# S5 head group: impulse responses on column quarters, spread through DRAM; state products ahead of time, shifted states in segments

## The chip, the cores and the metric

The kernel runs on one core of a Trainium2 chip. The time is the device time of one execution in microseconds. Before the change it is 2622.58 us, the median of three runs (2621.67 to 2623.46).

## The reference, cut to what matters

One layer of a streaming encoder for 384 tokens, a prompt of 256 and 8 running streams of 16: a SwiGLU feed-forward part (FFN), a mixer of two head groups, a second FFN, norms between. All of it is float32. The mixer projects the normed input once and splits the result into the SSD group (convolution, chunked scan) and the S5 group. The S5 group has 64 channel groups of 16 channels; each drives a complex diagonal state of 64 numbers:

```python
step = exp(log_step);  lb = exp((lam_re + 1j*lam_im) * step)      # 64 groups x 64 states
q    = (lb - 1) / lam                                              # zero-order hold
bu   = einsum('blgh,gnh->blgn', u, q[..., None] * b)
bu[:, 0] += lb * h0                                                # running streams have a state
h[t] = lb * h[t-1] + bu[t]                                         # associative scan over tokens
y    = real(einsum('blgn,ghn->blgh', h, c)) + d * u
```

The outputs are y, and the last state h of the prompt and of each stream. Then y goes through GELU, a gated linear layer and a norm into the output projection.

## The kernel before, in words

**The main products.** Every weight matrix is cut in blocks of 128 columns. `linear` (line 74) makes one output tile of 128 x 384. Its weights come in units of up to 8 blocks of 128 x 128: SP's queue loads `raw`, ScalarE rounds it to `wh` (line 55), VectorE makes the rest `wl` (line 56), and TensorE runs three products per block (lines 86 to 88). `raw` has four buffers, `wh` and `wl` three each. After every unit `c.tick()` is called.

**The FFN** (line 191) takes gate and up tiles in chunks of 11, 11, 11 and 10 for the first FFN. Per tile VectorE takes the gate product out (line 213), ScalarE applies SiLU (214), GpSimd multiplies by the norm factor (`f_g`, line 215), VectorE multiplies with the up product (218). After the tiles of a chunk come the down products (225), without GpSimd work.

**Work beside it.** `s5_prepare` (line 268) and `s5_run` (481) are generators, advanced by `tick`: at each third tick in the first FFN, from its chunk 1 on, at each tick in the mixer. That fixes the order in which instructions are traced. The order on each engine is then made by a planner that simulates the program with costs of its own: it takes the ready instruction that was traced earliest. So small operations that are ready early run long before their place in the trace, in gaps of their engine; but on the chip each engine and each queue works through its fixed order, and an instruction that waits holds up all behind it.

**s5_prepare** computes, from the parameters alone, the matrices of a scheme in steps of four tokens, in eight parts (`e`) of four groups of 128 rows (`l`), and puts them in DRAM: `s5m` holds per part five matrices, the two of the input side (`rt`, lines 453 to 457), the two of the output side (`cl`, 396 to 414), and the direct one (`tt`, 430 to 450): the effect of an input on the outputs of the same step of four tokens. For the direct one, `bbd` holds q times b as a block-diagonal operand, repeated for the four tokens, 128 columns wide; eight products per part (line 433) give the impulse responses for token distances 0 to 3, and ten multiply-adds on VectorE with a mask (447) put each at its place by distance. `s5e` holds the phases (`ph`, 459 to 477): powers of the unit numbers by doubling, on GpSimd, one buffer, stored by GpSimd's queue.

**s5_run** works part by part, `front(e)` and `back(e)`. `load_in` fetches the input matrices (`bdr`, one buffer) and the phases, `load_out` the output matrices (`bdo`, two buffers), all on SP's queue. In `front`, `px` (529) multiplies the input; VectorE turns it by the phases (549 to 554); GpSimd makes the decay mask `d0` (538) and the initial states times the fourth power, `lh` (547), and adds `lh` at the starts of the streams (558); VectorE scans (559); the result is turned back by products on VectorE (566) and GpSimd (567) and written to `hin` one step later (570, 571: one operation for the prompt and one for the streams); GpSimd takes out the last states, `fin` (572, 573), and puts zeros and initial states at the starts (574, 575). In `back`, `py` (582) multiplies the step inputs and `hin` by the output matrices, and ScalarE applies GELU. `psa` is a pool of four PSUM banks for all of this.

Of the kernel before, what the change touches and what calls it, by code (L numbers as in the profile page):

```python
# [267 lines left out]
def s5_prepare(c, a, late):  # L268
# [11 lines left out]
    c.s5e = c.dram.tile([8, P, 2, 4, 96], F32, name="s5_phases")  # L280
    with tc.tile_pool(name="s5p", bufs=1) as pool:
# [39 lines left out]
        l4 = c.const.tile([P, 32, 2], F32, name="s5l4")  # L321
        v.tensor_copy(l4[:, :, 0], lpr[:, :, 4])
        v.tensor_copy(l4[:, :, 1], lpi[:, :, 4])
        c.s5l4 = l4
# [52 lines left out]
        bbd = [t(f"bbd{i}", (P, 4, 2, 4, 16)) for i in range(2)]  # L377
        dd = t("dd", (P, 32))
        with tc.issue_after(late.ins):
            for i in range(2):  # L380
                gp.memset(bbd[i], 0.0)
            gp.dma_start(dd, a["s5d"])
        for e in range(8):
# [56 lines left out]
            tt = t("tt", (P, 4, 64))  # L440
            v.tensor_mul(
                tt, dd[:, ls].unsqueeze(2).to_broadcast([P, 4, 64]), c.ieq.unsqueeze(1).to_broadcast([P, 4, 64])
            )
# [15 lines left out]
            ph = t("ph", (P, 2, 4, 96))  # L459
# [12 lines left out]
            for z in (er, ei):  # L472
# [3 lines left out]
                )  # L476
            gp.dma_start(c.s5e[e], ph)
# [3 lines left out]
def s5_run(c, a, o, u, v5, gc):  # L481
# [10 lines left out]
    with tc.tile_pool(name="s5r", bufs=1, side="right") as pool:  # L492
# [4 lines left out]
        fin = pool.tile([P, 2, 32, 9], F32, name="s5fin")  # L497
# [11 lines left out]
        def load_in(e):  # L509
# [3 lines left out]
            phs[e] = pool.tile([P, 2, 4, 96], F32, tag="ph", name=f"ph{e}", bufs=2)  # L513
# [7 lines left out]
        def front(e):  # L521

            ls = slice(4 * e, 4 * e + 4)
            ph = phs[e]
            px = []
            for i in range(2):
# [11 lines left out]
            gp.tensor_mul(  # L538
                d0,
                c.s5dec[:, ls].unsqueeze(2).to_broadcast([P, 4, 96]),  # L540
                c.scanmask.unsqueeze(1).to_broadcast([P, 4, 96]),
            )
            lh = pool.tile([P, 2, 4, 8], F32, tag="lh", name=f"lh{e}")
            lt = pool.tile([P, 2, 4, 8], F32, tag="lt", name=f"lt{e}")
            l4 = [c.s5l4[:, ls, i].unsqueeze(2).to_broadcast([P, 4, 8]) for i in range(2)]
            he = [h0[:, i, ls, :] for i in range(2)]
            cmul(gp, lh[:, 0], lh[:, 1], he[0], he[1], l4[0], l4[1], lt[:, 0], lt[:, 1])
            gr, gi, a1, a2 = t("gr", 3), t("gi", 3), t("a1"), t("a2")
# [14 lines left out]
            hin = [t("gr", 3), t("gi", 3)]  # L563
            for i in range(2):
# [4 lines left out]
                hi4, b14, b24 = (z[:, :, 64:96].rearrange(smp, b=8) for z in (hin[i], b1, b2))  # L569
# [45 lines left out]
        nc.sync.dma_start(o["s5"], fin)  # L615
# [350 lines left out]
def trunk(ctx: ExitStack, tc: tile.TileContext, a, o):  # L966
# [23 lines left out]
    cst = c.const.tile([P, 684], F32, name="cst")  # L990
# [3 lines left out]
    c.smask, c.ieq, c.scanmask, c.seqm = cst[:, 512:516], cst[:, 516:580], cst[:, 580:676], cst[:, 676:684]  # L994
# [91 lines left out]
def _shape_constants():  # L1086
# [8 lines left out]
            (k // 16) % 4 == np.arange(4)[None, :],  # L1095
            k % 64 == np.arange(64)[None, :],
# [26 lines left out]
def layout(i):  # L1123
# [47 lines left out]
    d = a["s5_d"].reshape(32, 2, 16).transpose(1, 2, 0)  # L1171
    out["s5d"] = np.broadcast_to(d[:, None], (2, 4, 16, 32)).reshape(P, 32)
# [47 lines left out]
```

## Time and profile before

| | us |
|---|---|
| median of three runs | 2622.58 |
| the profiled execution | 2624.0 |
| its span, first to last instruction | 2622.2 |
| TensorE busy | 2570.5 |
| VectorE busy | 1387.7 |
| ScalarE busy | 926.5 |
| GpSimd busy | 658.8 |

The profile is of one execution. TensorE's mean granted clock over it is 0.991 of full speed. A product's record is longer than its share of the time, since products overlap: the main products are recorded with some 327 ns and begin every 0.16 us. Products of float32 operands that are not rounded, as in the S5 part, are two records each. The first FFN lasts to about 1060 us, the S5 parts run from 1160 to 1270 us.

### The profile page before, as it was taken

How to read it: one execution, taken by the hardware profiler on the slowest of the kernel's cores; microseconds unless marked ns; L12 is line 12 of the kernel's file. 1: busy time of each engine (PE TensorE's matmuls, PEld its weight loads, DVE VectorE, ACT ScalarE, POOL GpSimd, SP SyncE). 2: the span in 40 equal slices, each digit the busy share in tenths (PEclk: the TensorE clock that was granted, in tenths of full speed). 3: DMA queues.
4: the chain of work that ended last, by engine and by line, in shares of the span. 5: the costliest groups of instructions: out<-in, count | busy, mean ns of one | idle time of the engine just before them, and what ended most of it. 6: DMA issues, size and time to landing. Idle time of an engine off the chain costs nothing.

```text
span 2622.2 us, 39628 instructions
## 1 busy us (share of the span) xinstructions
PE 2570.5 (98%) x15873; PEld 2546.2 (97%) x15873; DVE 1387.7 (53%) x1964; ACT 926.5 (35%) x1180; POOL 658.8 (25%) x1012
## 2 busy tenths in 40 slices
PE   8989999999999999999899999999999999999997
PEld 8989999999999999988899999999999999999997
DVE  7744466564444445568878865444344444444443
ACT  6322332223323335332445644333223332233343
POOL 1573283121100003027566531100000010000112
PEclk9999999999999999999999999999999999999998
DMA  6444564454444436467455544444444444444443
GB/s 204 151 129 140 165 200 149 138 160 135 133 127 147 136 121 186 150 163 159 122 170 167 166 151 136 137 136 129 135 139 137 136 130 133 141 137 137 131 133 107
DMA packets 147001, 380.41 MB, mean 145 GB/s; under 512 B 46080, under 2 KB 51360, under 8 KB 146816
## 3 DMA queue, kind: packets, MB, share of 16 engines
q1 hardware_dynamic: 133456, 344.28, 43.3%
q0 software_dynamic: 11344, 30.72, 3.8%
q10 hardware_dynamic: 2016, 2.87, 0.3%
q8 instruction: 124, 2.03, 0.3%
q14 instruction: 61, 0.50, 0.1%
HBM read 354.60 MB, written 20.05 MB: 143 GB/s over the span
## 4 chain that ended last, share of the span: by engine, by line
PE 86%; DVE 6%; POOL 4%; issue 1%; DMA 1%; ACT 1%; SPq 0%; DVEq 0%; ACTq 0%; POOLq 0%
PE f_pd L86 9%; PE f_pd L88 9%; PE f_pd L87 9%; PE f_pg L86 8%; PE f_pg L87 8%; PE f_pg L88 8%; PE f_pu L88 8%; PE f_pu L86 8%; PE f_pu L87 8%; PE p L87 2%; PE p L86 2%; PE p L88 2%; DVE wl L56 2%; PE u L87 1%; PE u L88 1%
## 5 line engine op out<-in xcount | busy, mean ns | idle before, releaser
L55 ACT CAST wh<-raw 128x1024 fp32r<-128x1024 f32 (+3 forms) x668 | 658.4, 986 | 1450.9 <-PE f_pd L87 417.2
L56 DVE TENSOR_TENSOR wl<-raw,wh 128x1024 fp32r<-128x1024 f32 (+3 forms) x668 | 788.5, 1181 | 678.9 <-ACT wh L55 672.0
L88 PE MATMUL f_pu<-n_h,wl 128*128 128x384 f32 x1360 | 445.7, 328 | 8.1 <-DVE wl L56 8.1
L215 POOL TENSOR_TENSOR f_g<-f_g,n_r 128x384 f32<-128x384 f32 x86 | 130.4, 1516 | 1271.7 <-ACT f_g L214 1271.6
L86 PE MATMUL f_pd<-f_hh,wh 128*128 128x384 f32 x1376 | 448.1, 326 | 0.0
L87 PE MATMUL f_pd<-f_hl,wh 128*128 128x384 f32 x1376 | 448.1, 326 | 0.0
L88 PE MATMUL f_pd<-f_hh,wl 128*128 128x384 f32 x1376 | 448.1, 326 | 0.0
L86 PE MATMUL f_pg<-n_h,wh 128*128 128x384 f32 x1360 | 445.0, 327 | 2.6 <-DVE f_g L213 2.6
L86 PE MATMUL f_pu<-n_h,wh 128*128 128x384 f32 x1360 | 445.5, 328 | 0.0
L87 PE MATMUL f_pu<-n_l,wh 128*128 128x384 f32 x1360 | 445.1, 327 | 0.0
L87 PE MATMUL f_pg<-n_l,wh 128*128 128x384 f32 x1360 | 444.1, 327 | 0.0
L88 PE MATMUL f_pg<-n_h,wl 128*128 128x384 f32 x1360 | 444.0, 326 | 0.0
L88 PEld LDWEIGHTS f_pu<-n_h,wl 128*128 128x128 f32 x1360 | 258.5, 190 | 8.7 <-DVE wl L56 8.7
L86 PEld LDWEIGHTS f_pg<-n_h,wh 128*128 128x128 f32 x1360 | 257.5, 189 | 3.0 <-issue 2.9
L87 PEld LDWEIGHTS f_pd<-f_hl,wh 128*128 128x128 f32 x1376 | 260.0, 189 | 0.0
L88 PEld LDWEIGHTS f_pd<-f_hh,wl 128*128 128x128 f32 x1376 | 260.0, 189 | 0.0
L86 PEld LDWEIGHTS f_pd<-f_hh,wh 128*128 128x128 f32 x1376 | 260.0, 189 | 0.0
L86 PEld LDWEIGHTS f_pu<-n_h,wh 128*128 128x128 f32 x1360 | 258.5, 190 | 0.1
L87 PEld LDWEIGHTS f_pu<-n_l,wh 128*128 128x128 f32 x1360 | 258.4, 190 | 0.1
L87 PEld LDWEIGHTS f_pg<-n_l,wh 128*128 128x128 f32 x1360 | 257.6, 189 | 0.1
L88 PEld LDWEIGHTS f_pg<-n_h,wl 128*128 128x128 f32 x1360 | 257.6, 189 | 0.0
L218 DVE TENSOR_TENSOR f_h<-f_pu,f_g 128x384 f32<-128x384 f32 x86 | 47.8, 556 | 163.2 <-PE f_pu L88 121.4
(481 smaller groups left out, 3133.0 us busy)
## 6 DMA issues: line engine op xcount, KB each, us to landing
raw<-in_wg_dram SPq DMA_DIRECT2D x170, 512.0 KB, 3.6
raw<-in_wu_dram SPq DMA_DIRECT2D x170, 512.0 KB, 3.6
raw<-in_wd_dram SPq DMA_DIRECT2D x80, 448.0 KB, 3.4
raw<-in_win_dram SPq DMA_DIRECT2D x64, 512.0 KB, 4.0
raw<-in_wd_dram SPq DMA_DIRECT2D x80, 320.0 KB, 3.0
raw<-in_wd_dram SPq DMA_DIRECT2D x48, 384.0 KB, 3.2
raw<-in_wout_dram SPq DMA_DIRECT2D x32, 512.0 KB, 3.8
raw<-in_wd_dram SPq DMA_DIRECT2D x16, 512.0 KB, 3.5
```

The source lines that it names most:

```text
L55: nc.scalar.copy(wh[:, :nk, :], raw[:, :nk, :])
L56: nc.vector.tensor_sub(wl[:, :nk, :], raw[:, :nk, :], wh[:, :nk, :].bitcast(F32))
L86: nc.tensor.matmul(ps, wh[:, i, :], xh, start=first, stop=False)
L87: nc.tensor.matmul(ps, wh[:, i, :], xl, start=False, stop=False)
L88: nc.tensor.matmul(ps, wl[:, i, :], xh, start=False, stop=last)
L215: on_pool = nc.gpsimd.tensor_mul(g, g, r)
L218: nc.vector.tensor_mul(halves(h), straight(pu), halves(g))
```

## The change

The direct matrix: `bbd` is no longer repeated for four tokens, so each product has 32 columns of weights. The four groups of a part are put on the four column quarters of the array, and write the four quarters of the partitions of one PSUM bank. Two operations of VectorE take the result to `kt`, with the diagonal term for distance 0. GpSimd's queue stores `kt` in DRAM (`kd`), and after a yield eight transfers from DRAM to DRAM copy it to the places by distance in the direct matrix, which one transfer has filled with zeros ahead.

The state products: `lh` is made in `s5_prepare`, on GpSimd, from a load of the initial states, and travels as 8 more columns of the phases.

In `s5_run`: ScalarE makes `d0` in four operations per part; VectorE adds `lh`; `hin` has segments of five, the state before a step and the four of the step, so that one operation of VectorE per part writes all; ScalarE copies each last state of a segment to the start of the next, the initial states to the streams' starts, and the last states to `fin`, which has two buffers now and is stored part by part on SP's queue. `py` reads the first four of each segment.

```diff
@@ s5_prepare @@
-    c.s5e = c.dram.tile([8, P, 2, 4, 96], F32, name="s5_phases")
+    c.s5e = c.dram.tile([8, P, 2, 4, 104], F32, name="s5_phases")
...
-        bbd = [t(f"bbd{i}", (P, 4, 2, 4, 16)) for i in range(2)]
-        dd = t("dd", (P, 32))
+        bbd = [t(f"bbd{i}", (P, 4, 2, 16)) for i in range(2)]
+        dd = t("dd", (P, 8))
+        zero = t("zero", (P, 256))
...
+        gp.dma_start(
+            c.s5m[:, :, 4].rearrange("e p l x -> p e (l x)"), zero.unsqueeze(1).to_broadcast([P, 8, 256])
+        )
+        kd = c.dram.tile([8, P, 64], F32, name="k_dram")
         for e in range(8):
...
-                m4 = [mm[pr].unsqueeze(2).to_broadcast([64, 4, 4, 16]) for mm in m]
-                v.tensor_sub(bbd[0][pr, :, g], m4[0], m4[1])
-                v.tensor_add(bbd[1][pr, :, g], m4[2], m4[3])
+                v.tensor_sub(bbd[0][pr, :, g], m[0][pr], m[1][pr])
+                v.tensor_add(bbd[1][pr, :, g], m[2][pr], m[3][pr])
             yield
-            kp = c.psa.tile([P, 4, 64], F32, tag="aux", name=f"kp{e}")
-            for l in range(4):
-                for i in range(2):
+            kp = c.psa.tile([P, 512], F32, tag="aux", name=f"kp{e}")[:, :64]
+            for i in range(2):
+                for l in range(4):
                     nc.tensor.matmul(
-                        kp[:, l, :],
-                        bbd[i][:, l].rearrange("p g s h -> p (g s h)"),
+                        kp[32 * l : 32 * l + 32, :],
+                        bbd[i][:, l].rearrange("p g h -> p (g h)"),
...
-            for b in range(4):
-                for k in range(b + 1):
-                    dst = tt[:, :, 16 * b : 16 * b + 16]
-                    v.scalar_tensor_tensor(
-                        dst, kp[:, :, 16 * k : 16 * k + 16], c.smask[:, b - k : b - k + 1], dst, op0=ALU.mult, op1=ALU.add
-                    )
-            gp.dma_start(c.s5m[e, :, 4], tt)
-            yield
+            kt = t("kt", (P, 64), bufs=2)
+            v.scalar_tensor_tensor(kt[:, 0:16], c.ieq, dd[:, e : e + 1], kp[:, 0:16], op0=ALU.mult, op1=ALU.add)
+            v.tensor_copy(kt[:, 16:64], kp[:, 16:64])
+            gp.dma_start(kd[e], kt)
+            yield
+
+            for s in range(4):
+                for g in range(2):
+                    gp.dma_start(
+                        c.s5m[e, :, 4].rearrange("(g s h) l x -> g s l h x", g=2, s=4)[g, s][:, :, 16 * s :],
+                        kd[e].rearrange("(l g h) x -> g l h x", l=4, g=2)[g][:, :, : 64 - 16 * s],
+                    )
...
+            he = t("he", (P, 2, 4, 8))
+            gp.dma_start(he, a["s5h0"][:, :, ls, :])
+            l4 = [lp[:, ls, 4].unsqueeze(2).to_broadcast([P, 4, 8]) for lp in (lpr, lpi)]
+            cmul(gp, er[:, :, 96:], ei[:, :, 96:], he[:, 0], he[:, 1], l4[0], l4[1], y1[:, :, 0:8], y2[:, :, 0:8])
             gp.dma_start(c.s5e[e], ph)
@@ s5_run, front @@
-            gp.tensor_mul(
-                d0,
...
-            cmul(gp, lh[:, 0], lh[:, 1], he[0], he[1], l4[0], l4[1], lt[:, 0], lt[:, 1])
+            for l in range(4):
+                nc.scalar.activation(d0[:, l, :], c.scanmask, AF.Copy, scale=c.s5dec[:, 4 * e + l : 4 * e + l + 1])
...
-                gp.tensor_add(s0, s0, lh[:, i])
+                v.tensor_add(s0, s0, lh[:, i])
...
+            fin = pool.tile([P, 2, 4, 9], F32, tag="fin", name=f"fin{e}", bufs=2)
+            hin = [pool.tile([P, 4, 24, 5], F32, tag=f"h{i}", name=f"hin{e}_{i}", bufs=2) for i in range(2)]
+            seg = "p l (s k) -> p l s k"
             for i in range(2):
                 b1, b2 = t("a1"), t("a2")
                 v.tensor_mul(b1, hs[i], ph[:, 0])
                 gp.tensor_mul(b2, hs[1 - i], ph[:, 1])
...
-                v.tensor_tensor(hin[i][:, :, 1:64], b1[:, :, 0:63], b2[:, :, 0:63], op=op)
-                v.tensor_tensor(hi4[:, :, :, 1:4], b14[:, :, :, 0:3], b24[:, :, :, 0:3], op=op)
-                gp.tensor_tensor(fin[:, i, ls, 0:1], b1[:, :, 63:64], b2[:, :, 63:64], op=op)
-                gp.tensor_tensor(fin[:, i, ls, 1:9], b14[:, :, :, 3], b24[:, :, :, 3], op=op)
-                gp.memset(hin[i][:, :, 0:1], 0.0)
-                gp.tensor_copy(hi4[:, :, :, 0], h0[:, i, ls, :])
+                gp.memset(hin[i][:, :, 0, 0], 0.0)
+                nc.scalar.copy(hin[i][:, :, 16:24, 0], h0[:, i, ls, :])
+                v.tensor_tensor(hin[i][:, :, :, 1:5], b1.rearrange(seg, k=4), b2.rearrange(seg, k=4), op=op)
+                nc.scalar.copy(hin[i][:, :, 1:16, 0], hin[i][:, :, 0:15, 4])
+                nc.scalar.copy(fin[:, i], hin[i][:, :, 15:24, 4])
+            nc.sync.dma_start(o["s5"][:, :, ls, :], fin)
             return hin
@@ s5_run, back @@
-                for f, mv in ((2, v5[:, 4 * e + l, :]), (0, hin[0][:, l, :]), (1, hin[1][:, l, :])):
+                for f, mv in ((2, v5[:, 4 * e + l, :]), (0, hin[0][:, l, :, 0:4]), (1, hin[1][:, l, :, 0:4])):
```

The rest of the diff follows from this: the mask of the ten multiply-adds leaves the constants, `s5d` is laid out by channel, `s5l4` and the one store of `fin` at the end go.

## Rows read from the trace of the kernel before

**Rows 1.** The page, busy time of TensorE: us (share of span) xrecords.

```profile
PE 2570.5 (98%) x15873; PEld 2546.2 (97%) x15873; DVE 1387.7 (53%) x1964; ACT 926.5 (35%) x1180; POOL 658.8 (25%) x1012
```

**Rows 2.** Windows: length, busy us PE, PEld, DVE, ACT, POOL; clock, DMA share, GB/s.

```profile
1160.00:1280.00 120.00, 107.12 (x718) 104.39 (x717) 93.96 (x159) 37.51 (x46) 80.10 (x167) 0.96 0.69 153
100.00:203.00 103.00, 94.88 (x555) 94.29 (x554) 44.98 (x70) 29.45 (x36) 80.38 (x269) 0.95 0.44 142
203.00:1150.00 947.00, 947.00 (x5868) 943.52 (x5867) 492.11 (x675) 307.64 (x385) 199.93 (x264) 1.00 0.50 149
```

**Rows 3.** TensorE's waits, whole span: who for whom: total us, times, longest.

```profile
PE f_pu L88 <- DVE wl L56: 8.1, 2, 5.3
PE py L582 <- DVE gr L571: 5.0, 3, 1.9
...
PE px L529 <- DMA bdr<-s_mats: 4.0, 2, 2.0
```

**Rows 4.** Timeline of TensorE, one block of line 433: start, us, record, [idle before].

```profile
354.60 1.89 PE L433 MATMUL kp<-cl,bbd 128*128 128x64 f32 x16
356.31 0.41 PE L86 MATMUL f_pg<-n_h,wh 128*128 128x384 f32 x1
```

**Rows 5.** Timeline of TensorE, po products, and pd products on column halves.

```profile
1306.58 1.85 PE L814 MATMUL po<-ct,hT 128*128 128x16 f32 x16
1308.29 0.47 PE L815 MATMUL po<-ct,s 128*128 128x128 f32 x2
...
1320.20 0.88 PE L792 MATMUL pd<-lt,xdt 128*64 128x128 f32 x12
1321.01 0.43 PE L88 MATMUL xs<-n_h,wl 128*128 128x384 f32 x1
```

**Rows 6.** Groups by line, GpSimd's wb loads: busy us, mean ns, idle before.

```profile
L394 POOL DMA_DIRECT2D wb<-w_dram x32 | 19.7, 622 | 0.6 <-DMA w_dram<-ws 0.6
```

**Rows 7.** DMA issues, 40 to 700 us, tt's store: KB, us to landing.

```profile
s_mats<-tt POOLq DMA_DIRECT2D x8, 128.0 KB, 2.8
```

**Rows 8.** Timeline of ScalarE and of GpSimd at one f_g, FFN chunk 1.

```profile
365.13 0.53 ACT L214 ACTIVATE f_g<-f_g 128x384 f32<-128x384 f32 x1 [3.71 <-DVE f_g L213]
...
368.55 1.01 POOL L215 TENSOR_TENSOR f_g<-f_g,n_r 128x384 f32<-128x384 f32 x1
```

**Rows 9.** Timelines, FFN chunk 0: two f_g on ScalarE and GpSimd, phases, TensorE.

```profile
135.50 0.52 ACT L214 ACTIVATE f_g<-f_g 128x384 f32<-128x384 f32 x1
...
147.45 0.10 POOL L462 MEMSET ph<- 128x4 f32 x1 [2.10 <-DMA s_phases<-ph]
...
147.63 0.20 POOL L260 TENSOR_TENSOR ph<-ph,ur 128x4 f32<-128x4 f32 x1
...
150.43 0.99 POOL L215 TENSOR_TENSOR f_g<-f_g,n_r 128x384 f32<-128x384 f32 x1
...
171.82 0.53 ACT L214 ACTIVATE f_g<-f_g 128x384 f32<-128x384 f32 x1 [0.29 <-DVE f_g L213]
...
186.37 0.99 POOL L215 TENSOR_TENSOR f_g<-f_g,n_r 128x384 f32<-128x384 f32 x1
...
191.81 0.69 PE L88 MATMUL f_pu<-n_h,wl 128*128 128x384 f32 x1 [5.33 <-DVE wl L56]
```

**Rows 10.** Groups of GpSimd, 1160 to 1270 us, line 567.

```profile
L567 POOL TENSOR_TENSOR a<-gr,ph 128x384 f32<-128x384 f32 x8 | 10.3, 1293 | 0.8 <-DVE gr L571 0.3
...
L567 POOL TENSOR_TENSOR a<-gi,ph 128x384 f32<-128x384 f32 x8 | 8.3, 1037 | 1.7 <-DVE gi L559 1.7
```

**Rows 11.** Groups of VectorE, 1160 to 1270 us, line 570.

```profile
L570 DVE TENSOR_TENSOR gr<-a,a 128x252 f32<-128x252 f32 x8 | 7.6, 952 | 9.1 <-POOL a L567 9.1
...
L570 DVE TENSOR_TENSOR gi<-a,a 128x252 f32<-128x252 f32 x8 | 3.3, 418 | 2.8 <-POOL a L567 2.6
```

**Rows 12.** Timeline of ScalarE, a small cast.

```profile
1154.95 0.24 ACT L670 CAST dar<-da 128x48 fp32r<-128x48 f32 x1 [0.38 <-DVE da L666]
```

**Rows 13.** Timeline of SP's queue, eight gc transfers.

```profile
1199.45 6.26 SPq L591 DMA_DIRECT2D gc<-gv  x8
```

More of the change, by code (lines that the diff above doesn't have):

```diff
@@ L320, in s5_prepare @@
         c.s5dec = dec
[L321 to L324, printed above, removed]
         qr, qi, den, nr = t("qr"), t("qi"), t("den"), t("nr")
@@ L381, in s5_prepare @@
                 gp.memset(bbd[i], 0.0)
+            gp.memset(zero, 0.0)
             gp.dma_start(dd, a["s5d"])
+        gp.dma_start(
+            c.s5m[:, :, 4].rearrange("e p l x -> p e (l x)"), zero.unsqueeze(1).to_broadcast([P, 8, 256])
+        )
+        kd = c.dram.tile([8, P, 64], F32, name="k_dram")
         for e in range(8):
@@ L457, in s5_prepare @@
             gp.dma_start(c.s5m[e, :, 0:2].rearrange("p f l n -> p f (l n)"), rt)
-            ph = t("ph", (P, 2, 4, 96))
+            ph = t("ph", (P, 2, 4, 104))
             y1, y2 = t("y1", (P, 4, 32)), t("y2", (P, 4, 32))
@@ L496, in s5_run @@
             gp.memset(z, 0.0)
-        fin = pool.tile([P, 2, 32, 9], F32, name="s5fin")
         h0 = pool.tile([P, 2, 32, 8], F32, name="s5h0")
@@ L512, in load_in @@
                 nc.sync.dma_start(bdr[0][pr, :, :, g, :].rearrange(mats), c.s5m[e, pr, 0:2].rearrange(mats))
-            phs[e] = pool.tile([P, 2, 4, 96], F32, tag="ph", name=f"ph{e}", bufs=2)
+            phs[e] = pool.tile([P, 2, 4, 104], F32, tag="ph", name=f"ph{e}", bufs=2)
             nc.sync.dma_start(phs[e], c.s5e[e])
@@ L523, in front @@
             ls = slice(4 * e, 4 * e + 4)
-            ph = phs[e]
+            ph, lh = phs[e][:, :, :, :96], phs[e][:, :, :, 96:]
             px = []
@@ L537, in front @@
             d0 = t("d0")
-            gp.tensor_mul(
-                d0,
[L540 to L546, printed above, removed]
-            cmul(gp, lh[:, 0], lh[:, 1], he[0], he[1], l4[0], l4[1], lt[:, 0], lt[:, 1])
-            gr, gi, a1, a2 = t("gr", 3), t("gi", 3), t("a1"), t("a2")
+            for l in range(4):
+                nc.scalar.activation(d0[:, l, :], c.scanmask, AF.Copy, scale=c.s5dec[:, 4 * e + l : 4 * e + l + 1])
+            gr, gi, a1, a2 = t("gr"), t("gi"), t("a1"), t("a2")
             v.tensor_mul(gr, px[0], ph[:, 0])
@@ L562, in front @@
                 hs.append(gg)
-            hin = [t("gr", 3), t("gi", 3)]
+            fin = pool.tile([P, 2, 4, 9], F32, tag="fin", name=f"fin{e}", bufs=2)
+            hin = [pool.tile([P, 4, 24, 5], F32, tag=f"h{i}", name=f"hin{e}_{i}", bufs=2) for i in range(2)]
+            seg = "p l (s k) -> p l s k"
             for i in range(2):
@@ L568, in front @@
                 op = ALU.subtract if i == 0 else ALU.add
-                hi4, b14, b24 = (z[:, :, 64:96].rearrange(smp, b=8) for z in (hin[i], b1, b2))
-                v.tensor_tensor(hin[i][:, :, 1:64], b1[:, :, 0:63], b2[:, :, 0:63], op=op)
-                v.tensor_tensor(hi4[:, :, :, 1:4], b14[:, :, :, 0:3], b24[:, :, :, 0:3], op=op)
-                gp.tensor_tensor(fin[:, i, ls, 0:1], b1[:, :, 63:64], b2[:, :, 63:64], op=op)
-                gp.tensor_tensor(fin[:, i, ls, 1:9], b14[:, :, :, 3], b24[:, :, :, 3], op=op)
-                gp.memset(hin[i][:, :, 0:1], 0.0)
-                gp.tensor_copy(hi4[:, :, :, 0], h0[:, i, ls, :])
+                gp.memset(hin[i][:, :, 0, 0], 0.0)
[4 more added lines that the diff above has]
+            nc.sync.dma_start(o["s5"][:, :, ls, :], fin)
             return hin
@@ L614, in s5_run @@
                 yield
-        nc.sync.dma_start(o["s5"], fin)
     c.ssd_pool = c.ssd_stack.enter_context(tc.tile_pool(name="ssd", bufs=1, side="right"))
@@ L989, in trunk @@
         nc.tensor.matmul(idle[:, :P], c.ones, c.ones, start=True, stop=True)
-    cst = c.const.tile([P, 684], F32, name="cst")
+    cst = c.const.tile([P, 632], F32, name="cst")
     tri = c.tmp.tile([P, T], F32, tag="sq", name="tri", bufs=3)[:, :256]
@@ L993, in trunk @@
     c.mask3 = cst[:, 128:512].rearrange("p (i x) -> p i x", i=3)
-    c.smask, c.ieq, c.scanmask, c.seqm = cst[:, 512:516], cst[:, 516:580], cst[:, 580:676], cst[:, 676:684]
+    c.ieq, c.scanmask, c.seqm = cst[:, 512:528], cst[:, 528:624], cst[:, 624:632]
     c.supr = c.const.tile([P, P], F32R, name="supr")
@@ L1094, in _shape_constants @@
             up, up, us,
-            (k // 16) % 4 == np.arange(4)[None, :],
-            k % 64 == np.arange(64)[None, :],
+            k % 16 == np.arange(16)[None, :],
             np.broadcast_to((np.arange(96) % 4 != 0) & (np.arange(96) >= 64) | (np.arange(96) > 0) & (np.arange(96) < 64), (P, 96)),
@@ L1170, in layout @@
     out["s5bt"] = bt.transpose(2, 0, 1, 3, 4)
-    d = a["s5_d"].reshape(32, 2, 16).transpose(1, 2, 0)
-    out["s5d"] = np.broadcast_to(d[:, None], (2, 4, 16, 32)).reshape(P, 32)
+    out["s5d"] = a["s5_d"].reshape(8, P).T
     out["s5h0"] = np.stack([_lanes(a["state_s5_re"]), _lanes(a["state_s5_im"])], 1)
```

3 lines of the change are left out of this document (removed).

## The prediction

> **What bounds the kernel now.** First the busy shares: TensorE works 2570.5 of 2622.2 us [rows 1], so what counts is the 52 us in which it stands still and what its own instructions take. Then the stretches, by the table of windows: from 203 to 1150 us TensorE is busy throughout at full clock, and it is not in two others [rows 2]. From 100 to 203 us (first FFN, chunk 0, while s5_prepare runs beside it) 94.88 of 103 us are busy at a mean granted clock of 0.95; from 1160 to 1280 us (s5_run beside the projections of z, bt, ct, xs) 107.12 of 120 us at 0.96. An idle us costs one us, a stretch at the lower of the two clock levels half its length. So the first stretch loses 8.1 + 0.05 x 103 = 13.3 us, the second 12.9 + 0.04 x 120 = 17.7 us. TensorE's waits give the causes [rows 3]: in the first it waits for wl from VectorE (8.1 us), in the second mostly for the shifted states of s5_run (5.0) and for the transfer into the single input matrix (4.0). The rest of the 52 us lies at the start and the end, which the change does not touch.
>
> Whatever TensorE saves in the full stretch comes off the time directly: nothing else is near its limit there (VectorE 492 of 947 us, ScalarE 308, GpSimd 200).
>
> **The change part by part.**
>
> *Impulse responses on quarters.* Eight blocks of 8 products, 16 records each, lie in the full stretch. One block: it starts at 354.60 and the next main product starts at 356.31, 1.71 us for 16 records of 128 columns of weights and 64 of data, 107 ns each [rows 4]. After, the same 16 records carry 32 columns of weights. The trace has no quarter; it has halves: the pd products, 64 columns of weights and 128 of data, in two column halves, take 12 records from 1320.20 to 1321.01, 67 ns each, changes of shape at both ends included [rows 5]. The number of data columns does not set the pace: 16 po records with 16 columns of data take 1.71 us too, from 1306.58 to 1308.29 [rows 5]. Upper bound of the cost 107 ns (a quarter pays like the whole: gain 0), then 67 ns (16 x 67 = 1.07 us, gain 0.64 us a block), lower bound a quarter of 107, 27 ns (0.43 us, gain 1.28 us). I take 47 ns, midway between the half's row and that lower bound, since the weights are half of that row's: 0.75 us, gain 0.96 us a block, 8 x 0.96 = 7.7 us, between 0 and 10.2.
>
> The Trainium skill (TensorEngine Tiling (Array Packing), Overview, Key Properties) says that changing the tiling mode drains the engine, which speaks against eight short blocks inside long runs of whole-array products. The pd rows hold two such changes and still come out at 67 ns; if each change cost another 0.2 us, an estimate in the size of one product, the gain would be 4.5 us in place of 7.7.
>
> *VectorE in s5_prepare.* Ten masked multiply-adds and a product into tt become one multiply-add and a copy; the block-diagonal operand shrinks by four. This is cheaper, and VectorE is not what ends the stretch: nothing gained, nothing lost.
>
> *The spread in DRAM.* For each of 8 blocks one store of kt (in place of that of tt) and 8 more transfers on GpSimd's queue, once a memset and a zero fill: 64 x 0.62 us, the row of the similar wb loads [rows 6], 40 us in all, 5 us a block. The spreads wait for the store to land, 2.8 us by the row of tt's store [rows 7], and on GpSimd a waiting instruction holds up f_g (line 215), which the FFN needs. So f_g can come 8 us later once every 48 us or so. At the busiest place it now starts 2.9 us after ScalarE is done with it (365.66 to 368.55) [rows 8]; 2.9 + 8 = 11 us is still under the lag at which TensorE stops (below). I take 0; without that slack some 5 us.
>
> *State products and h0 moved into s5_prepare.* Eight loads of he and 8 x 6 small products join the phase chains of 92 to 220 us, together with a wider ph. Per chain: 0.62 us for the issue [rows 6], six products of 0.20 us [rows 9], 1.8 us. The chains already make f_g late: ScalarE is done at 136.02, f_g starts at 150.43; done at 172.35, starts at 186.37, and at 191.81 TensorE starts again after 5.33 us of waiting [rows 9]. So a lag of 14 us is where it stops. A chain ends with the store of ph, and the next waits 2.10 us for it [rows 9]; he has one buffer too, so its next load can be issued right behind the last product, in that gap, and has the whole next chain, some 13 us, to land. Left over are about 1.2 us a chain. Six chains lie before 203 us, 7 us of added GpSimd work; the order of GpSimd's queue is fixed ahead by the planner, which knows that work and will put f_g earlier among it, so only a part shows as lag. I take +2 us; bounds -6 (f_g falls between two chains) and +7 for the work alone.
>
> *s5_run.* GpSimd is busy 80.1 us of the 120 [rows 2]. The scan mask product, the six products of lh, the two additions at the sequence starts, the four fin operations and the copies of h0 leave it; what stays are the two products at line 567, 10.3 + 8.3 us [rows 10], and two memsets. VectorE stood 9.1 + 2.8 us before the subtraction and addition at line 570 [rows 11], almost all of it for GpSimd. With GpSimd at about 21 us this goes down to the product's own length. VectorE takes over 16 additions of 32 elements, some 0.2 us each by the small rows of GpSimd and ScalarE, and loses one of two operations per part (lines 570 and 571): about even. ScalarE takes ten small instructions per block, 80 x 0.24 us by a row of 48 elements [rows 12], 19 us on top of 37.5 of 120; queued behind them are the casts wh that TensorE's main products wait for, three buffers ahead. The py products read the states four of every five elements, which I take at nothing, as the main products read their data in a turned order too (line 84) and come every 0.16 us; at worst they pay like the doubled time of the 8 x 16 records of states, 14 us, which only a slower reading of strides could bring. SP gets one store of fin per block, and the weight loads stand behind it; SP is already held 6.26 us by eight gc transfers [rows 13]. So a part of the stall moves: TensorE will wait for the input matrix and for ScalarE's copy of the shifted states. Of 17.7 us lost I take half, 9 us; bounds: a loss of 6 us (the 5.0 us of waits for the states stay and ScalarE's copies add to them) and a gain of 17.7.
>
> **Sum.** The profiled execution took 2624.0 us. 2624.0 - 7.7 - 9 + 2 = 2609.3; the median of the three runs, 2622.6, lies 1.4 us under it, so 2608.
>
> **The rivals.**
>
> 1. *s5_run stays as slow.* The px products wait for a bdr that one buffer allows only after the last px, SP works through its list, VectorE is busy 94 of 120 us [rows 2]. For it: 4.0 us of waits on that load today; against it: most of VectorE's idle time is for GpSimd. Then -7.7 + 2: 2617.
>
> 2. *The quarters pay as the whole.* For it: the trace has no product of 32 columns beside another of its kind, and fewer data columns bring nothing; against it: the halves' 67 ns [rows 5]. Then -9 + 2: 2616. Both rivals at once: about 2625.
>
> 3. *GpSimd becomes the limit of the first FFN, the slower side.* Place: the chains up to 203 us. If the planner puts each he load so that GpSimd waits for it, 2.8 us more by the nearest landing, a chain grows by 1.8 + 2.8 = 4.6 us and the plan does not count on it; over the six chains before 203 us that is 28 us, all of it on TensorE since f_g is at the limit today: 2622.6 - 7.7 - 9 + 28 = 2634. It decides as soon as f_g starts over 14 us late in each FFN tile of that chunk. Against it: the single buffer lets the load go a chain ahead.
>
> 4. *It does not do what it says* would show as the spread DMAs waiting for one another, 8 x 2.8 us a block: f_g 22 us late once per block, 8 us over the limit, eight times: 64 us, 2672. The destinations are rows that do not overlap, so I give it little.
>
> **How the numbers follow.** Forecast 0.45, rival 1 0.24, rival 2 0.10, both 0.09, rival 3 0.09, rival 4 0.03. About what a measurement of this kernel can tell from no change is 0.2%, 5.2 us. Under 2617.3 lie the forecast and most of rivals 1 and 2, 0.71; over 2627.8 rivals 3 and 4 and a small part of the double failure, 0.13; the rest, 0.16, is no change. The range: the forecast's own bounds (quarters down to -10.2, s5_run to -15, the first FFN to -3) reach 2595; upward it takes in rivals 1, 2 and both together: 2626.
>
> **What would show it.** Line 433's heir in blocks of well under 1 us between two main products; in s5_run GpSimd under 30 us, VectorE's idle time before the subtraction gone, TensorE's idle time there near 6 us; f_g starts between 100 and 203 us no more than 14 us behind ScalarE, or else TensorE's waits for wl above 8.1 us. I am wrong if the clock falls more often in the first 203 us, or if TensorE waits in s5_run for wh behind ScalarE's copies.

## The result and the profile after

The changed kernel takes 2597.38 us (median of four runs, 2597.09 to 2599.15), the kernel before beside it 2623.02: ratio 0.9898, 95% interval 0.9886 to 0.9911. The forecast of 2608 had the sign, the range of 2595 to 2626 holds the time; the gain is 25.6 us where 14.7 were forecast.

The profiled execution went from 2624.0 to 2599.15 us, its span from 2622.2 to 2597.2. First the page and three stretches of the changed kernel, which answer to [rows 1, 2]; the last window starts 15 us earlier than in the kernel before, as its first px products do.

```profile
PE 2554.8 (98%) x15873; PEld 2528.8 (97%) x15873; DVE 1338.9 (52%) x1890; ACT 945.3 (36%) x1262; POOL 671.8 (26%) x1014
```

```profile
100.00:203.00 103.00, 97.83 (x592) 96.51 (x591) 44.95 (x75) 31.40 (x39) 90.23 (x282) 0.99 0.47 148
203.00:1135.00 932.00, 932.00 (x5828) 925.67 (x5827) 452.21 (x597) 305.10 (x380) 250.96 (x367) 1.00 0.51 151
1145.00:1265.00 120.00, 113.28 (x773) 111.45 (x771) 98.32 (x169) 64.24 (x134) 37.08 (x57) 0.97 0.78 174
```

GpSimd is busier in the first stretch (90.23 us, before 80.38), and yet TensorE loses less there: 5.2 us idle and 0.01 of the clock, 6 us in place of 13.3. In s5_run GpSimd fell from 80.1 to 37.1 us, ScalarE rose from 37.5 to 64.2, and TensorE loses 6.7 us idle and 3.6 by the clock, 10.3 in place of 17.7. TensorE's waits, over the whole span:

```profile
PE px L536 <- DMA bdr<-s_mats: 6.6, 5, 3.4
PE p L786 <- POOL xw L762: 5.4, 3, 4.0
...
PE f_pd L86 <- ACT f_hh L221: 3.0, 1, 3.0
...
PE f_pu L88 <- DVE wl L56: 2.1, 2, 1.1
```

VectorE's groups from 1145 to 1255 us hold one that answers to [rows 11], GpSimd's two that answer to [rows 10]:

```profile
L573 DVE TENSOR_TENSOR hin<-a,a 128x384 f32<-128x384 f32 x16 | 8.9, 554 | 6.8 <-POOL a L569 5.8 <-POOL hin L571 0.9
```

```profile
L569 POOL TENSOR_TENSOR a<-gr,ph 128x384 f32<-128x384 f32 x8 | 10.4, 1304 | 5.1 <-DVE hin L573 5.1
L569 POOL TENSOR_TENSOR a<-gi,ph 128x384 f32<-128x384 f32 x8 | 10.2, 1273 | 32.5 <-DVE gi L558 25.9 <-issue 6.6
```

GpSimd now waits for VectorE (25.9 us); VectorE waits 6.8 us for GpSimd, before 11.9. Of [rows 3] TensorE's waits for the states are gone, those for wl are down from 8.1 to 2.1, those for bdr are up from 4.0 to 6.6. What none of these views says is how much time each stretch gained. For that the two traces are laid beside each other at three places that do the same work in both: the first transposition wT (after FFN chunk 0), the first product of u (after the first FFN), the first product of the output projection on y (after S5 and SSD). TensorE's timelines, the kernel before and then the changed one:

```profile
307.58 0.27 PE L355 MATMUL wT<-cst,wr 128*128 128x128 f32 x1
...
1051.39 0.33 PE L86 MATMUL u<-n_h,wh 128*128 128x384 f32 x1
...
1463.74 0.73 PE L86 MATMUL p<-y_h,wh 128*128 128x384 f32 x1
```

```profile
302.99 0.27 PE L351 MATMUL wT<-cst,wr 128*128 128x128 f32 x1
...
1037.40 0.33 PE L86 MATMUL u<-n_h,wh 128*128 128x384 f32 x1
...
1439.26 0.73 PE L86 MATMUL p<-y_h,wh 128*128 128x384 f32 x1
```

The differences to the kernel before in us, the stretches each from one profiled execution, with the experiments told below:

| kernel | median (us) | ratio, 95% interval | to wT | wT to u | u to y | rest |
|---|---|---|---|---|---|---|
| changed | 2597.38 | 0.9898 (0.9886 to 0.9911) | -4.6 | -9.4 | -10.5 | -0.6 |
| quarters alone | 2614.08 | 0.9967 (0.9955 to 0.9978) | +1.1 | -9.4 | -1.5 | -1.1 |
| longer chains alone | 2612.12 | 0.9955 (0.9940 to 0.9970) | -4.0 | +0.9 | -7.6 | -0.6 |
| new s5_run alone | 2614.35 | 0.9967 (0.9954 to 0.9980) | +0.1 | +1.2 | -9.6 | -1.1 |
| before, chains held | 2610.74 | 0.9951 (0.9937 to 0.9964) | -13.4 | 0.0 | +0.7 | -0.6 |
| short chains held, rest changed | 2592.20 | 0.9872 (0.9856 to 0.9889) | -13.2 | -9.4 | -8.8 | -0.9 |

The three parts of the sum were -7.7 (quarters), +2 (first FFN), -9 (s5_run). All three came out better, and the one with the wrong sign is the largest difference: 6.6 of the 10 us.

TensorE's timeline of one impulse response block of the changed kernel, which answers to [rows 4]:

```profile
349.85 0.33 PE L88 MATMUL f_pg<-n_h,wl 128*128 128x384 f32 x1
350.10 0.43 PE L436 MATMUL kp<-cl,bbd 128*32 128x64 f32 x16
350.46 0.43 PE L86 MATMUL f_pg<-n_h,wh 128*128 128x384 f32 x1
```

The 16 records take 0.36 us in place of 1.71, 22 ns each, below the prediction's lower bound of 27. The first comes 0.25 us behind the product before it, where products otherwise follow every 0.16.

GpSimd's timeline at one f_g of FFN chunk 0, changed kernel:

```profile
147.60 0.58 POOL L485 DMA_DIRECT2D s_phases<-ph  x1
148.19 1.02 POOL L215 TENSOR_TENSOR f_g<-f_g,n_r 128x384 f32<-128x384 f32 x1
150.83 0.10 POOL L466 MEMSET ph<- 128x4 f32 x1 [1.62 <-DMA s_phases<-ph]
```

All six f_g from 113 us on stand like this, right behind the issue of a store, and run while it lands. In [rows 9] the f_g at 150.43 stands behind 19 instructions of the next chain.

### The profile page after: what moved, and what is told of

Its sections match the earlier page's. It is cut to its first block, busy times and chain, and to the rows that moved or that the text cites. A ratio compares the mean times of both kernels' runs of the same rounds, so it can differ in the third digit from the quotient of the medians.

```text
span 2597.2 us, 39630 instructions
## 1 busy us (share of the span) xinstructions
PE 2554.8 (98%) x15873; PEld 2528.8 (97%) x15873; DVE 1338.9 (52%) x1890; ACT 945.3 (36%) x1262; POOL 671.8 (26%) x1014
## 4 chain that ended last, share of the span: by engine, by line
PE 86%; DVE 5%; POOL 3%; DMA 2%; SPq 1%; ACT 1%; issue 1%; ACTq 0%; DVEq 0%; POOLq 0%
PE f_pd L88 9%; PE f_pd L87 9%; PE f_pd L86 9%; PE f_pg L86 8%; PE f_pg L87 8%; PE f_pg L88 8%; PE f_pu L87 8%; PE f_pu L86 8%; PE f_pu L88 8%; PE p L87 2%; PE p L88 2%; PE p L86 2%; DVE wl L56 1%; DMA bdr<-s_mats 1%; PE u L88 1%
## 5 line engine op out<-in xcount | busy, mean ns | idle before, releaser
L56 DVE TENSOR_TENSOR wl<-raw,wh 128x1024 fp32r<-128x1024 f32 (+3 forms) x668 | 779.8, 1168 | 694.8 <-ACT wh L55 687.3
```

Source lines behind the costliest of these rows:

```text
L56: nc.vector.tensor_sub(wl[:, :nk, :], raw[:, :nk, :], wh[:, :nk, :].bitcast(F32))
```

## The experiments

**Each part alone.** The quarters with their spread, and the s5_run of before; the longer chains without either; the new s5_run, with the products of lh still made there on GpSimd.

```
quarters alone:      ph (P, 2, 4, 96), no he; s5_run as before
longer chains alone: ph (P, 2, 4, 104), he and its cmul in s5_prepare;
                     s5_run: lh = phs[e][:, :, :, 96:], no cmul
new s5_run alone:    s5_prepare as before; s5_run new, with cmul(gp, lh ...)
```

> The kernel before with the impulse responses on quarters and the spread in DRAM alone; the phase chains and s5_run are those of before. Theory: the quarters save what the trace of after shows, 1.2 us in each of 8 blocks, all of it in the full stretch, and nothing moves in the first FFN: 2623.0 - 9.6 = 2613.4 us, the tile wT near 307.6 us as before, TensorE's wait for wl still near 8 us. Rival A: the quarters part also shifts the planner's order in the first FFN, and the 4.7 us gained there belong to it: 2608.7. Rival B: the 64 spread transfers on GpSimd cost something that the other parts give back: above 2616.

Measured 2614.08 us. The stretch from wT to u is 9.41 us shorter, as in the changed kernel, and wT lies at 308.69. The theory holds in the time and the stretch; neither rival does. But the first FFN did not stay quite as it was: GpSimd's order moved there too, wT comes 1.1 us later and TensorE waits 11.3 us for wl. TensorE is busy throughout from 203 us to u, so the 64 spread transfers cost it nothing.

> The kernel before with the state products in the phase chains of s5_prepare alone; kp as before, s5_run as before except that the products of lh on GpSimd are gone. Theory: the longer chain lets f_g fall between two chains, where the store of the phases has to land anyway, so the first FFN gets 4.7 us shorter (wT near 303 us, lags of f_g of 12 us at most); in s5_run GpSimd loses 27 us of its 80, which gives 2 to 5 us: 2613 to 2617. Rival A: the chain work costs the 2 us of the prediction, and the first FFN's gain came from another part: wT at 309 us or later, 2620 to 2625. Rival B: the products of lh were all of the trouble in s5_run: 2623.0 - 4.7 - 10.7 = 2607.6.

Measured 2612.12 us, wT at 303.55, lags of f_g 11.8 us at most: the first FFN's gain comes with the longer chains. The gain in s5_run is larger than expected, 7.6 us.

> The kernel before with the new s5_run alone (scan mask and boundary copies on ScalarE, additions at the sequence starts on VectorE, shifted states in segments); the products of lh stay on GpSimd in s5_run, the quarters and the longer chains are left out. Theory: GpSimd is so much emptier that the products of lh no longer reach VectorE: 9 to 11 us of s5_run's gain are there, 2612 to 2614, waits of py for VectorE gone, waits of px for bdr 5 to 7 us. Rival A: the products of lh on GpSimd were what VectorE waited for: 2618 to 2621, VectorE still idle before line 570's heir by 8 us or more. Rival B: ScalarE's eighty small copies cost as much as they save without the other parts: 2621 or more.

Measured 2614.35 us with 9.6 us gained in the stretch of S5; TensorE's waits for the states are gone and those for bdr are 8.8 us. This is the theory's time. But VectorE still stands before the subtraction and addition, in this kernel 10.9 us, almost as long as before (9.1 + 2.8 us, [rows 11]):

```profile
L570 DVE TENSOR_TENSOR hin<-a,a 128x384 f32<-128x384 f32 x16 | 9.0, 563 | 10.9 <-POOL a L566 9.9 <-POOL hin L568 1.1
```

So rival A had the row right and the time wrong: that idle time is not what the gain hung on. The two partial reliefs give 7.6 and 9.6 us and together 10.5, so either takes most of it. In both, the wait for bdr is then TensorE's largest from u to y (5.7 and 8.8 us).

**What a quarter costs.** The products of blocks 1 to 6 in other forms:

```
 if 1 <= e <= 5: order (l, i) in place of (i, l)
 e == 2: out = kp[0:32, 64*l : 64*l+64], w = bbd[i][:, l]
 e == 3: out = kp[64*(l%2) : +64, 64*(l//2) : +64], w = two l of bbd[i]
 e == 4: out = kp[0:64, 64*l : 64*l+64],  w = two l of bbd[i]
 e == 5: out = kp[:, 64*l : 64*l+64],  w = bbd[i]
 e == 6: all products twice
```

> The changed kernel with another form of the eight products in blocks 1 to 6 (the matrix that leaves the block is wrong in blocks 1 to 6): block 0 and 7 as they are (four quarters in turn), 1 the same quarter twice running, 2 one quarter for all, 3 the two halves two products at a time, 4 one half for all, 5 the whole 128 columns, 6 the quarters with every product twice. Theory: a quarter is cheap because neighbours in other quarters run beside one another: block 0 16 records in 0.36 us, block 1 about 0.6, block 2 as slow as the whole, near 107 ns a record (1.7 us), block 3 near 0.9, block 4 near 1.7, block 5 1.71 us, block 6 0.36 us more than block 0. Rival: the price goes by the columns loaded, no matter where: block 1 and 2 like block 0, block 3 and 4 near 0.7 to 1.1 us, block 5 1.71.

TensorE's timeline, the main product ahead, the block and the one behind, for one quarter (block 2), one half (4), the whole (5) and the quarters doubled (6):

```profile
443.92 0.33 PE L88 MATMUL f_pg<-n_h,wl 128*128 128x384 f32 x1
444.17 1.08 PE L454 MATMUL kp<-cl,bbd 128*32 128x64 f32 x16
445.18 0.43 PE L86 MATMUL f_pg<-n_h,wh 128*128 128x384 f32 x1
...
515.36 1.15 PE L454 MATMUL kp<-cl,bbd 128*64 128x64 f32 x16
516.44 0.43 PE L86 MATMUL f_pd<-f_hh,wh 128*128 128x384 f32 x1
...
549.53 0.33 PE L88 MATMUL f_pg<-n_h,wl 128*128 128x384 f32 x1
549.69 1.89 PE L454 MATMUL kp<-cl,bbd 128*128 128x64 f32 x16
551.39 0.41 PE L86 MATMUL f_pg<-n_h,wh 128*128 128x384 f32 x1
...
598.12 0.33 PE L88 MATMUL f_pg<-n_h,wl 128*128 128x384 f32 x1
598.37 0.65 PE L454 MATMUL kp<-cl,bbd 128*32 128x64 f32 x32
598.96 0.43 PE L86 MATMUL f_pg<-n_h,wh 128*128 128x384 f32 x1
```

One execution, 2603.36 us; only the blocks are read from it. Neither the theory nor the rival has it all. In one quarter 16 records take 1.01 us, in one half 1.08, in the whole 1.70: a narrow product costs some 60% of a wide one, changes of shape included, and 32 columns hardly less than 64. Only four quarters in turn bring it to 0.36 (block 0; block 1, with every quarter twice running, 0.38), and 16 more records on them cost 0.22 us, 14 ns each. So of the 0.62 us between the two main products around a block, 0.16 is what they take without one, 16 x 14 ns = 0.22 the products, and 0.24 is left. It is put down to the two changes of shape: ahead of the narrow blocks 0.25 us pass, ahead of the whole one 0.16. What the change behind a block takes was not measured by itself.

The planner cut block 3, the two halves, into pieces of 8, 4 and 4 records:

```profile
467.81 0.46 PE L454 MATMUL kp<-cl,bbd 128*64 128x64 f32 x8
468.19 0.43 PE L86 MATMUL f_pd<-f_hh,wh 128*128 128x384 f32 x1
...
468.72 0.45 PE L454 MATMUL kp<-cl,bbd 128*64 128x64 f32 x4
469.09 0.43 PE L88 MATMUL f_pd<-f_hh,wl 128*128 128x384 f32 x1
```

In the kernel's order the 8 are four on either half, and each 4 are on one half. The 8 take 0.38 us and the 4 take 0.37: the second half costs next to nothing beside the first.

**Only the longer chain, its results unused.**

```
+ he, sc = t("he", (P, 2, 4, 8)), t("sc", (P, 2, 4, 8))
+ gp.dma_start(he, a["s5h0"][:, :, ls, :])
+ cmul(gp, sc[:, 0], sc[:, 1], he[:, 0], he[:, 1], l4[0], l4[1], ...)
```

> The kernel before with each phase chain of s5_prepare lengthened by the load of he and the six small products, whose results go nowhere; s5_run, kp and the width of the stored phases as before. Theory: the added work itself makes the first FFN shorter, because with it the order of GpSimd's queue has each f_g between two chains and no later: wT 3 to 5 us earlier, lags of f_g of 12 us at most, total 2618 to 2620 although only work was added. Rival: the gain of ph_alone before wT came from something else (the phases' width, the missing work later), and the longer chain costs its 1.7 us or more: wT at or after that of before, 2623 to 2630.

Measured 2629.39 us, ratio 1.0019 (1.0009 to 1.0028), wT 5.0 us later than before: the theory falls, the rival's time is right. But the order of GpSimd's queue was not that of the changed kernel. The store does not need the unused products, so the planner puts some of them behind it, and f_g falls into the next chain as before. GpSimd's timeline, the store and the f_g behind it:

```profile
181.88 0.59 POOL L481 DMA_DIRECT2D s_phases<-ph  x1
...
186.04 0.10 POOL L462 MEMSET ph<- 128x4 f32 x1 [2.40 <-DMA s_phases<-ph]
...
189.67 0.98 POOL L215 TENSOR_TENSOR f_g<-f_g,n_r 128x384 f32<-128x384 f32 x1
```

**A second buffer for the phases; bdr on another queue.**

```
- ph = t("ph", (P, 2, 4, 104))
+ ph = t("ph", (P, 2, 4, 104), bufs=2)
- nc.sync.dma_start(bdr[0] ...)      in load_in(e + 1)
+ gp.dma_start(bdr[0] ...)           in front(e), behind the px products
```

> The changed kernel with two buffers for the phases in s5_prepare, so that no chain waits for the store of the one before (1.1 to 2.9 us each today). Theory: GpSimd paces the first FFN, six gaps of 1 to 3 us go, f_g falls behind by less, TensorE's waits for wl and f_hh (2.1 + 3.0 us) shrink and a clock fall goes: 2591 to 2595. Rival A: the planner puts more chain work ahead of f_g into the freed time, as in the kernel before, and nothing is gained or 2 to 4 us are lost: 2597 to 2601. Rival B: GpSimd no longer paces, 2597 whatever it does.

Measured 2611.17 us, ratio 0.9947 (0.9931 to 0.9964): taking the wait away lost 14 us. Rival A had the mechanism, but foresaw a loss of 4 us at most. With the gap gone the planner put up to 12.8 us of the next chain ahead of f_g, and the load of he, issued at a chain's end, now had to be waited for; GpSimd's timeline:

```profile
182.93 0.58 POOL L485 DMA_DIRECT2D s_phases<-ph  x1
...
187.03 0.25 POOL L260 TENSOR_TENSOR ph<-he,lpr 128x32 f32<-128x32 f32 x1 [3.14 <-DMA he<-in_s5h_dram]
...
195.69 1.00 POOL L215 TENSOR_TENSOR f_g<-f_g,n_r 128x384 f32<-128x384 f32 x1
```

How far f_g starts behind the issue of the last store (us, the six tiles from 113 us on), and the stretch to wT:

| kernel | chains | f_g behind the store | to wT |
|---|---|---|---|
| before | short | 0.6, 0.6, 5.7, 6.1, 8.7, 11.8 | 0 |
| quarters alone | short | 0.6, 5.7, 6.9, 10.0, 11.7, 12.9 | +1.1 |
| changed, longer chains alone | long | 0.6 in all six | -4.6, -4.0 |
| only the longer chain | long | before it, 1.8, 1.8, 4.9, 7.8, 8.3 | +5.0 |
| second buffer for ph | long | 0.9, 4.6, 4.5, 7.7, 12.8, 11.1 | +9.9 |

Among chains of one length the traces order themselves by this place; across lengths they do not. With its results unused, the longer chain has its f_g less far behind than quarters alone and is 3.9 us later at wT.

> The changed kernel with the loads of bdr issued on GpSimd's queue right behind the px products instead of SP's. Theory: what is left of the stall in s5_run (px waits 6.6 us for bdr) is the place in SP's list, behind gc, fin and raw: waits for bdr at most 2 us, total 2590 to 2594. Rival: the transfer engines are full there (97% busy from 1190 to 1229 us) and the load lands no earlier: waits for bdr 5 us or more, 2596 to 2599.

Measured 2597.68 us, ratio 0.9897 (0.9882 to 0.9911). The waits for bdr went from 6.6 to 3.4 us and the stretch of S5 is 1.7 us shorter in the profiled execution, but the median shows no difference: the rival's time, with its sign (waits of 5 us or more) missing. Whether the rest is SP's order or the transfers themselves is open. Both edits together gave 2612.44 us, 0.9953 (0.9937 to 0.9969), as the second buffer alone.

> Both of these edits together. Theory: they lie in different stretches and add up: between 2584 and 2590. Rival: one of them does nothing: 2591 to 2597.

**The place of f_g held.** Each chain from the second to the seventh is put behind the f_g that is due when it starts. The first is put behind the first f_g and the eighth behind that of the seventh, which moves little: the first store leaves at 112.46 us, before at 112.65. Nothing else is changed.

```
+ c.fgs = getattr(c, "fgs", []) + [on_pool]        # in the first FFN, per tile
+ with tc.issue_after(c.fgs[min(4 + e, 10) if e else 0].ins):
      gp.memset(er[:, :, 0:1], 1.0)
      gp.memset(ei[:, :, 0:1], 0.0)
```

> The kernel before with one thing alone: the first two memsets of phase chain 1 to 6 are put behind f_g 5 to 10 in GpSimd's queue, so that no part of a chain goes ahead of the f_g that is due (in the kernel before, f_g 7 to 10 stand 40, 18, 30 and 36 instructions into the next chain). No work is added or taken away. Theory: the place of f_g, not the length of the chain, is what the first FFN's gain hangs on: f_g 0.6 us behind each store, lags of 12 us at most, wT 4 to 6 us earlier, 2617 to 2620. Rival: the changed chain's own work did it, and the kernel before stays where it was, 2621 to 2625; or the rest of the chain, put later, is late for something else: above 2625.

Measured 2610.74 us. The theory is right, and its size was too small: all six f_g start 0.6 us behind a store, lags are 9.4 us at most, and the stretch to wT is 13.4 us shorter, all that TensorE lost there. (The counts in the expectation are off: the trace has 19, 20, 30 and 38.) The window, and two rounds of GpSimd:

```profile
100.00:203.00 103.00, 103.00 (x636) 103.00 (x635) 51.83 (x78) 33.51 (x42) 85.43 (x269) 1.00 0.49 157
```

```profile
144.62 0.59 POOL L480 DMA_DIRECT2D s_phases<-ph  x1 [0.30 <-POOL ph L267]
145.23 1.02 POOL L215 TENSOR_TENSOR f_g<-f_g,n_r 128x384 f32<-128x384 f32 x1
147.31 0.11 POOL L465 MEMSET ph<- 128x4 f32 x1 [1.05 <-DMA s_phases<-ph]
...
159.92 0.59 POOL L480 DMA_DIRECT2D s_phases<-ph  x1 [0.30 <-POOL ph L267]
160.53 1.01 POOL L215 TENSOR_TENSOR f_g<-f_g,n_r 128x384 f32<-128x384 f32 x1
```

One chain with its f_g takes 15.3 us (144.62 to 159.92). ScalarE hands over an f_g every 15.6 us in this kernel (line 214 at 135.28, 150.88, 166.48), so GpSimd keeps up. In the changed kernel a round takes 17.0 us, and it does not:

```profile
164.60 0.57 POOL L485 DMA_DIRECT2D s_phases<-ph  x1
165.19 1.02 POOL L215 TENSOR_TENSOR f_g<-f_g,n_r 128x384 f32<-128x384 f32 x1
...
181.46 0.57 POOL L485 DMA_DIRECT2D s_phases<-ph  x1
182.05 1.02 POOL L215 TENSOR_TENSOR f_g<-f_g,n_r 128x384 f32<-128x384 f32 x1
```

With the same place of f_g, then, the longer chains cost 8.9 us (wT at 302.99 against 294.14). These two kernels differ in the quarters and in s5_run too; the last kernel below has both as the changed one, short chains and wT at 294.42, which makes it 8.6.

> The changed kernel with two buffers for the phases in s5_prepare, as the run that lost 14 us, and the chains put behind f_g as in the kernel above. Theory: that loss was the place of f_g alone; with the place held, the gaps of 1 to 3 us before each chain go, the chain with its f_g takes about 15.2 us, under the 15.6 us in which TensorE does an FFN tile, so that lags stay under 10 us and TensorE's waits for wl and f_hh go: 3 to 5 us under the changed kernel, ratio to before 0.988 to 0.989 (about 2592 to 2595). Rival: the place is held but the second buffer brings nothing, 2596 to 2599.

Measured 2600.53 us, ratio 0.9911 (0.9897 to 0.9924): the theory falls. Holding the place took back 11 of the 14 us, but wT is 5 us later than in the changed kernel. The first products with he now stand between store and f_g and wait 1 us for the load, so that five of the six f_g come 2.0 to 4.1 us behind the store and a round takes 17.4 us. The single buffer of ph had been hiding the landing of he.

> The same with the loads of bdr on GpSimd's queue. Theory: 1 to 2 us less than the kernel above, as the profiled execution of that edit alone had it (the px waits 3.4 in place of 6.6 us). Rival: no difference, as the median of that edit alone had it.

Measured 2602.61 us, 0.9918 (0.9904 to 0.9931): no difference, as the rival says, though the waits for bdr fell from 4.9 to 1.8 us.

**Quarters, new s5_run, short chains held.** The state products go back to s5_run; the lines are those of the new s5_run alone and of the place held, above.

> The changed kernel without its state products in the phase chains (they are made in s5_run on GpSimd, as before the change) and with each chain put behind its f_g: quarters, new s5_run, short chains, place held. Theory: the three gains stand side by side: first FFN 13.4 us (as with the place held in the kernel before), quarters 9.4, s5_run 8 to 10 (as with the new s5_run alone): 2624 - 31 to 33 = 2591 to 2593, ratio 0.987 to 0.9885, faster than the changed kernel. Rival: the state products on GpSimd in s5_run come back as a stall of VectorE once everything else is earlier: 2597 to 2600, no better than the changed kernel.

Measured 2592.20 us (2591.03 to 2592.53), ratio 0.9872 (0.9856 to 0.9889), as the theory says. The span of the profiled execution, 2590.0 us, is 32.2 shorter than that of before; the three terms from three other kernels, 13.4, 9.4 and 9.6, sum to 32.4. It lies 5.2 us under the changed kernel's median; the two were measured in different sets of runs, and the intervals of their ratios overlap by a little (0.9886 to 0.9889).

## Why the prediction was right, and where it was not

*Quarters, forecast -7.7, measured -9.4.* The gain lies between the bounds, but the reasoning behind 47 ns does not hold: it scaled the price with the columns of weights, and one quarter by itself (1.01 us for 16) costs hardly less than one half (1.08, the 67 ns of the half's row). What makes quarters cheap is that four of them run beside one another, and the pd rows gave no sign of that. So the term came near for another reason than the one given. The lower bound of the cost was not one: 22 ns a record in a block, and 14 for 16 further records, where 27 was the least. The Trainium skill states a drain at each change of mode (TensorEngine Tiling (Array Packing), Tiling Modes, Key Properties; the prediction names the section wrongly). What is left over agrees with it: 0.24 us a block for both changes where the estimate had 0.4, some 2 us in all. The same section says that tiles load and multiply in parallel, and this case's 1.01 us in one quarter against 0.36 in four agrees. Seven blocks save 1.25 us each, and the one that the planner cuts in two, and which so pays for the changes twice, saves 0.93; that makes 9.7 us, where the stretch got 9.4 shorter.

*VectorE in s5_prepare and the spread, forecast 0.* Right: the stretch from wT to u gains the same 9.4 us in every kernel with all blocks on quarters. The spread's lag was foreseen well too: at the place of [rows 8], f_g now comes 10.8 us behind ScalarE (357.19 to 368.02 us), where 11 was said and before it was 2.9, and TensorE does not stop.

*State products in the chains, forecast +2, measured -4.6.* This is the step that failed: "a lag of 14 us is where it stops", with the added work going on top. No such limit shows. In the changed kernel no lag before 203 us is over 11.6 us, and yet TensorE waits 5.1 us there, with tile after tile late; a single one behind the spread, 10.8 us here and 11.7 in quarters alone, costs nothing. What counts is the place of f_g in the chain and the length of a round. In the kernel before four of the six f_g stood 5.7 to 11.8 us behind the store. The planner fixes that place from times of its own; with the longer chain it happened to put all six between two chains. The prediction had this as its bound of -6 ("f_g falls between two chains"), but the sum did not go by it and no row spoke for it, so the better sign is luck. And the work's own price was larger than the 7 us that were its bound: 8.9 us at equal place, because 17.0 us a round is over the 15.6 in which TensorE needs an f_g, while the short chain's 15.3 is under it. The round is longer by 1.7 us and not by the 1.2 that were "left over": the issue of he's load does not fall into the gap behind the store but stands ahead of it. The -4.6 is the difference of a place worth 13.4 and work that costs 8.9. The same work with its results unused, its f_g not between the chains, cost 5.0 us, so the gain isn't the work's own. The planner's rule itself was not looked into, so which edit tips it can't be told ahead.

One more thing is part of a round. Some of the chain's small operations are recorded with 1.2 us in place of 0.2. From GpSimd's timeline of the changed kernel, and from VectorE's:

```profile
152.90 0.20 POOL L264 TENSOR_TENSOR y<-ph,ur 128x4 f32<-128x4 f32 x1
153.04 1.25 POOL L263 TENSOR_TENSOR ph<-he,lpi 128x32 f32<-128x32 f32 x1
```

```profile
152.98 1.21 DVE L56 TENSOR_TENSOR wl<-raw,wh 128x1024 fp32r<-128x1024 f32 x1
```

Between 112 and 190 us there are 12 of them, over two a round, and each ends within 0.2 us behind the end of one of VectorE's operations on wl (line 56); in the kernel with the place held it is 12 of 12 too. Other small ones beside such operations keep their 0.2 us. So a round seems to hang on VectorE's work as well; no run here changed that, and the cause stays open.

*s5_run, forecast -9, measured -10.5 up to the projection on y.* The sum came near. In the 120 us that it was worked out for, the loss fell by 7.4 us, from 17.7 to 10.3; the rest of the 10.5 lies elsewhere between u and y. Over that whole stretch TensorE's idle time fell from 20.1 to 13.5 us, and its busy time by 3.8. Of the signs named some came: TensorE idle 6.7 us in the 120 (near 6), waits for the input matrix in place of those for the states, none for wh. GpSimd is at 37.1 us where under 30 was said. The reason was only partly right: VectorE's idle time before the subtraction is 6.8 us now, not gone, and the kernel with the new s5_run alone kept 10.9 of it and gained 9.6. What went is TensorE's wait for the finished states. Which of the moved instructions is worth how much was not separated, and the stretch differs between kernels with the same s5_run (-10.1 with the second buffer for ph, -14.2 with the chains held as well), so that some us of it may be its meeting with other work.

*The rivals and the range.* 1 and 2 did not come. 4 did not either. 3, GpSimd as the limit of the first FFN by a wait for he, was given little since the load has "the whole next chain" to land. In the changed kernel its first use comes early in the next chain, and f_g and the wait for the store lie between; the second buffer for ph brought that wait (up to 3.1 us) into the open. The three bounds under the range add up to 2594.4, not 2595; the measured time lies 2.4 us above the lower end, as all three terms came out better than forecast.

## What to carry to other kernels

When a second engine's chain shares an in-order queue with something that the bottleneck waits for, read two numbers from the trace: how far into the chain that instruction stands, and whether one round is shorter than the bottleneck's own. Here the first was worth 13 us and the second 9, and both were larger than what the added work looked like. Hold the place by an explicit order, then judge the work. A wait that seems idle may be what covers a landing or holds an order, as the second buffer for ph showed.

## What the runs showed of the hardware

Products with 32 or 64 columns of weights on one part of the array cost about the same, 1.01 and 1.08 us for 16 records, against 1.70 for 128 columns; on four quarters in turn 0.36. On two halves, 8 records take 0.38 us where 4 on one half take 0.37. The 16 x 8 records of the states, read four of every five elements, took 274 ns each against 286 and 278 before, and within a block they begin every 112 ns in both kernels: such a stride costs nothing there. Some small GpSimd operations are recorded with 1.2 us in place of 0.2 and end with one of VectorE's on wl.
